# Operands of the seven products formed once and kept in DRAM, gate's elementwise work on VectorE, and a block's final norm in the next block

## The chip, the cores and the metric

One core of one Trainium2 chip. The metric is device time in microseconds of one execution of the program; the time given for the kernel before is the median of three runs. The engines are named as in the profile: PE (TensorE: matmuls; PEld is its weight loads), DVE (VectorE), ACT (ScalarE), POOL (GpSimd) and SP (SyncE, which here issues every DMA). Each engine runs its own instructions in order and waits on semaphores for the others.

## The reference

One layer of a streaming encoder over 2048 prompt frames and 64 frames of a running stream, model width 1024, feed-forward width 2816, all in float32. Retention heads and forgetting-attention heads work on one input projection; their outputs meet in one output projection. What matters here is what follows it:

```python
x = x + jnp.einsum('btc,cd->btd', mix, w_out)
h = _rmsnorm(x, g_ffn)
g = jnp.einsum('btd,df->btf', h, w_gate)
u = jnp.einsum('btd,df->btf', h, w_up)
x = x + jnp.einsum('btf,fd->btd', jax.nn.silu(g) * u, w_down)
y = _rmsnorm(x, norm_final_gain)
```

for 2048 + 64 frames.

## The kernel before

**Precision.** A float32 matrix is kept as two parts, `hi` (a cast on ACT) and `lo` (the rest, a subtraction on DVE); the helper `split` (L83) issues both. A product is three matmuls: hi·hi, hi·lo, lo·hi. Since `split` is a helper, all casts stand at L85 and all subtractions at L86 of the profile; the tile names tell them apart. All DMAs are issued in `dma`, L48, on SP's queue.

**Seven products.** Gate and up, `h @ w_gate` and `h @ w_up`, are not formed with eight products of half-size blocks but with seven, in the manner of Strassen and Winograd. The tokens of a block are cut into two halves, the 1024 input features into two halves, and a weight's columns into two halves. From the quarters b11, b12 (first 512 features, first and second half of the tokens), b21, b22 (the other 512 features) seven right-hand operands are made: b11, b12 - b11 = t1, b22 - t1 = t2, b22 - b12, t2 - b21, b21 and b22; from the weight's quarters seven left-hand operands likewise (`prep`, L1068). The seven results are added up in PSUM and on DVE into the four quarters of the output.

**Stages.** The program first runs the input projection and both kinds of heads. Then comes the *output projection* (`p3_stream`): a loop over 17 tiles of 128 tokens (the last has 64). For tile i it loads the mixer's output `m` and the softmax sums `rb`, splits them, does 48 matmuls with the resident `w_out`, adds `x`, stores the sum as `x1_d`, forms the norm `h`, and one tile later (`back`, L550) transposes `h` eight times on PE into `hT` (bufs 2), which is stored as one 512 KB piece in `h2_d`. It is interleaved with attention up to about 1432 us and runs alone from there to about 1581 us.

Beside its second half, `prefetch` (L1044) brings the operands of the first FFN block into SBUF: in four steps, each of which loads two pieces of `h2_d`, forms t1, t2 and two differences on DVE and POOL (L1023 to L1030), and splits the seven operands for one of four groups of 128 features into `hb`, which holds all seven operands, hi and lo. A step is issued when a given tile of the output projection has been issued (`p3_done`: 6, 8, 10, 12; then the first weights at 14). Its buffers are the two of tag `raw` in pool `ws`, which the output projection's `m` and `rb` use too.

The *FFN* goes over three blocks of 768, 768 and 576 tokens (`BLOCKS`), and in each over 11 passes (`NP`) of 256 of the 2816 columns. Pass i is

- gate, `gu(i, 0)`: seven products of 12 matmuls each; `prep` is called four products ahead and makes the weights' operands: three sums when a weight tile is new (L1079 to L1081), one more at the fourth product (L1084), all on POOL, and a split for each product;
- down of the pass before, `down(i - 1)`: for each half of the 1024 output columns, for each tile of 128 tokens, six matmuls and an addition to `y` on DVE (L1183);
- up, `gu(i, 1)`: as gate; its outputs are multiplied with gate's `G` and split into `act`, the input of down.

In `out` (L1125) a quarter of up's output is finished in four links: DVE adds PSUM to a partial sum (L1134), POOL multiplies with `G` (L1135), ACT casts to `act`, DVE subtracts. The first product of each gate or up part is copied out of PSUM by ACT (L1156); the third accumulates on the same PSUM buffer and must wait for that copy.

In the last pass of a block the operands of the next block are loaded and formed as in `prefetch`, from four buffers, and then the last down runs; its second half ends for each tile with `finish` (L1188): the final norm (square and sum on ACT, two small operations on POOL, scale on DVE), the output's DMA. `hb` has one buffer, so the new operands are written after the last product of the old block. The next block's `y` tiles (6 buffers) are loaded after its first gate part.

The order of the instructions on each engine is laid out by the framework when the program is built: it may move an instruction ahead of one written earlier where its inputs and its buffer are there sooner. So in the trace the next block's first gate products stand between the matmuls of the last down.

Of the kernel before, what the change touches and what calls it, by code (L numbers as in the profile page):

```python
# [16 lines left out]
D = 1024  # L17
# [21 lines left out]
def hybrid_kernel(ctx: ExitStack, tc: tile.TileContext, a: dict):  # L39
# [18 lines left out]
    h2_d = tc.dram_tile([128, KT, TP], F32, name="h2_d")  # L58
# [449 lines left out]
    def p3_stream(last):  # L508

        m_t, mT_t, x_t, h_t, rb_t = {}, {}, {}, {}, {}  # L510

# [38 lines left out]
        def back(i):  # L550
# [8 lines left out]
            dma(h2_d[:, :, i * 128:(i + 1) * 128], hT)  # L559
            p3_done.add(i)  # L560

# [443 lines left out]
    def load_h(n, raws):  # L1005

        t0, nt = BLOCKS[n]
        hf = nt // 2
        hb = hb_t[n] = hp.tile([128, 7, 2, 4, HALF], F32R, tag="hb", name="hb")
        for k in range(4):  # L1010
            r = []
            for e in range(2):
                raw = raws()[:, 0:nt]
                dma(raw, h2_d[:, 4 * e + k, t0:t0 + nt])
                r += [raw[:, 0:hf], raw[:, hf:nt]]
            b11, b12, b21, b22 = r
            t1 = hp.tile([128, HALF], F32, tag="t1", name="t1")[:, 0:hf]
            t2 = hp.tile([128, HALF], F32, tag="t2", name="t2")[:, 0:hf]

            def put(j, src):  # L1020
                split(hb[:, j, 0, k, 0:hf], hb[:, j, 1, k, 0:hf], src)

            ve.tensor_tensor(t1, b12, b11, op=ALU.subtract)  # L1023
            ge.tensor_tensor(b12, b22, b12, op=ALU.subtract)
            ve.tensor_tensor(t2, b22, t1, op=ALU.subtract)
            put(0, b11)
            put(2, b21)
            put(4, t1)
            put(1, t2)
            ge.tensor_tensor(b21, t2, b21, op=ALU.subtract)  # L1030
            put(3, b12)
            put(6, b22)
            put(5, b21)
            yield
# [9 lines left out]
    def prefetch():  # L1044

        for n, _ in enumerate(load_h(0, lambda: ws.tile([128, D], F32, tag="raw", name="raw"))):
            yield 8 + 2 * n
        load_w(0, 0, ws)
        yield 14
# [9 lines left out]
    with tc.tile_pool(name="fw", bufs=1, reuse_waits="tile") as fw, \  # L1059
# [8 lines left out]
        def prep(x):  # L1068
# [6 lines left out]
            if j == 0:  # L1075
# [3 lines left out]
                ge.tensor_tensor(s1, r1[:, lo], r1[:, hi], op=ALU.add)  # L1079
                ge.tensor_tensor(s2, s1, r0[:, lo], op=ALU.subtract)  # L1080
                ge.tensor_tensor(r1[:, lo], r0[:, lo], r1[:, lo], op=ALU.subtract)  # L1081
# [205 lines left out]
```

## Time and profile before

| | |
|---|---|
| median of three runs | 3120.7 us (3119.35 to 3123.26) |
| the profiled execution | 3118.12 us, its span 3116.3 us |
| granted TensorE clock, mean | 0.984 |
| instructions | 45009 |
| output projection alone on the chip | about 1436 to 1581 us |
| FFN, first and last gate or up matmul | 1580.7 to 3086 us |

In the profile, a line of the timeline has the start, the duration (in us), the engine, the line of the kernel, the operation and its output and inputs by name; in brackets the idle time of that engine just before and what ended it. A row of a stretch (A:B) has the stretch's length and the busy time of each engine with its number of instructions, then the granted clock, the share of DMA time and GB/s. A row of a group has the number of instructions, their total, the mean in ns, and the idle time before them with its cause.

### The profile page before, as it was taken

What the parts mean: (1) busy time and instruction counts of PE and PEld (TensorE: products, weight loads), DVE (VectorE), ACT (ScalarE), POOL (GpSimd) and SP (SyncE); (2) the same over time, 40 slices, a digit from 0 to 9 for tenths busy, and PEclk for the clock granted to TensorE, in tenths of its full rate; (3) what the DMA queues carried; (4) which work ended last, traced back from release to release, by engine and by line L of the source; (5) the groups of instructions that cost most, each with busy time, mean ns of one, the idle gap of its engine ahead of it and who ended that gap; (6) DMA issues with size and microseconds to landing.
All of it is one profiled execution on the core that took longest, in us unless ns stands there. A gap on an engine that the chain in (4) does not pass through costs nothing. (4 is left out here: it accounts for less than half of the span.)

```text
span 3116.3 us, 45009 instructions
## 1 busy us (share of the span) xinstructions
PE 2953.4 (95%) x16684; PEld 2645.7 (85%) x16684; DVE 1976.0 (63%) x3661; ACT 1252.3 (40%) x2662; POOL 707.6 (23%) x804
## 2 busy tenths in 40 slices
PE   8999899999999999898889999998999999899997
PEld 8999778788888888777679998987888998788886
DVE  4233554477766677665446766769666676877776
ACT  4233332265655556554332322324233233433332
POOL 0000111111111111000132323324233232433332
PEclk9999999999999999999989999999999999899999
DMA  7565633332422223544652222225212221522221
GB/s 200 168 183 169 172 97 108 100 104 77 131 84 72 60 85 118 155 123 137 188 176 62 68 68 61 75 61 170 81 55 74 64 66 56 168 82 83 87 82 51
DMA packets 415261, 328.91 MB, mean 106 GB/s; under 512 B 22346, under 2 KB 361674, under 8 KB 415042
## 3 DMA queue, kind: packets, MB, share of 16 engines
q1 hardware_dynamic: 415042, 326.05, 34.9%
q8 instruction: 131, 2.15, 0.3%
q14 instruction: 88, 0.72, 0.1%
HBM read 246.81 MB, written 79.17 MB: 105 GB/s over the span
## 5 line engine op out<-in xcount | busy, mean ns | idle before, releaser
L1153 PE MATMUL mm<-hb,w 128*128 128x384 f32 (+1 forms) x5544 | 926.8, 327 | 75.5 <-ACT U L1156 45.4
L1153 PEld LDWEIGHTS mm<-hb,w 128*128 128x128 f32 x5544 | 903.2, 191 | 98.8 <-ACT U L1156 54.3
L1182 PE MATMUL dn<-wd,act 128*128 128x512 f32 (+1 forms) x2244 | 518.8, 391 | 4.4 <-ACT act L85 3.9
L1182 PEld LDWEIGHTS dn<-wd,act 128*128 128x128 f32 (+1 forms) x2244 | 413.4, 185 | 99.7 <-ACT act L85 5.6
L492 PE MATMUL mm<-w,hT 128*128 128x512 f32 x1632 | 445.8, 408 | 0.7 <-DVE hT L86 0.5
L86 DVE TENSOR_TENSOR w<-raw,w 128x512 fp32r<-128x512 f32 (+1 forms) x358 | 346.4, 988 | 80.2 <-ACT w L85 76.9
L1183 DVE TENSOR_TENSOR y<-y,dn 128x512 f32<-128x512 f32 (+1 forms) x374 | 255.5, 686 | 202.8 <-PE dn L1182 202.5
L492 PEld LDWEIGHTS mm<-w,hT 128*128 128x128 f32 x1632 | 291.3, 190 | 56.3 <-issue 2.2
L232 PE MATMUL mm<-w,hT 128*128 128x386 f32 x1632 | 298.8, 342 | 0.9 <-ACT hT L85 0.9
L85 ACT CAST w<-raw 128x512 fp32r<-128x512 f32 (+1 forms) x358 | 220.6, 643 | 195.2 <-PE mm L1153 98.5
L232 PEld LDWEIGHTS mm<-w,hT 128*128 128x128 f32 x1632 | 288.6, 190 | 1.9 <-ACT hT L85 1.5
L85 ACT CAST wd<-rawd 128x512 fp32r<-128x512 f32 x132 | 75.4, 618 | 394.0 <-PE dn L1182 381.3
L872 ACT ACTIVATE P<-P,nm 128x512 f32<-128x512 f32 (+3 forms) x288 | 189.6, 661 | 96.2 <-DVE nm L866 95.9
L567 PE MATMUL mm<-w,mT 128*128 128x512 f32 x816 | 210.3, 407 | 3.1 <-ACT mT L85 1.8
L86 DVE TENSOR_TENSOR lo<-t,hi 128x512 fp32r<-128x512 f32 (+1 forms) x288 | 183.0, 655 | 44.2 <-ACT hi L85 42.4
L85 ACT CAST hi<-t 128x512 fp32r<-128x512 f32 (+1 forms) x288 | 154.6, 562 | 139.8 <-PE t L889 136.0
L567 PEld LDWEIGHTS mm<-w,mT 128*128 128x128 f32 x816 | 152.8, 193 | 36.6 <-ACT mT L85 2.2
L1135 POOL TENSOR_TENSOR G<-G,T 128x384 f32<-128x384 f32 (+1 forms) x33 | 32.7, 992 | 627.0 <-DVE T L1134 627.0
L889 PE MATMUL t<-ident,P 128*128 128x128 f32 x1088 | 160.1, 276 | 15.3 <-DVE lo L86 9.1
L86 DVE TENSOR_TENSOR act<-G,act 128x384 fp32r<-128x384 f32 (+1 forms) x132 | 133.9, 1014 | 51.0 <-ACT act L85 50.3
L889 PEld LDWEIGHTS t<-ident,P 128*128 128x128 f32 x1088 | 128.3, 142 | 37.0 <-DVE lo L86 13.8
L377 POOL TENSOR_TENSOR qk<-t,t 128x256 f32<-128x256 f32 x34 | 24.8, 729 | 592.2 <-DVE t L374 285.4
(231 smaller groups left out, 4060.5 us busy)
## 6 DMA issues: line engine op xcount, KB each, us to landing
raw<-w_gate SPq DMA_DIRECT2D x66, 512.0 KB
raw<-w_up SPq DMA_DIRECT2D x66, 512.0 KB
rawd<-w_down SPq DMA_DIRECT2D x66, 512.0 KB
hf<-hT_d SPq DMA_DIRECT2D x34, 512.0 KB
qk_d<-qkT SPq DMA_DIRECT2D x32, 512.0 KB
KA<-qk_d SPq DMA_DIRECT2D x72, 128.0 KB
V<-v_d SPq DMA_DIRECT2D x36, 256.0 KB
hT_d<-hf SPq DMA_DIRECT2D x17, 512.0 KB
```

Source lines behind the costliest of these rows:

```text
L85: se.copy(hi, src)
L86: ve.tensor_tensor(lo, src, f32(hi), op=ALU.subtract)
L232: te.matmul(ps, hT[:, u, k], w[:, v, k], start=n == 0, stop=n == 23)
L377: ge.tensor_tensor(qk[:, :, 0], t1[:, :, 0], t2[:, :, 1], op=ALU.subtract)
L492: te.matmul(ps, hT[:, u, k], w[:, v, k], start=k == 0 and j == 0, stop=k == 7 and j == 2)
L567: te.matmul(ps, mT[:, u, k], mix_w[4 + c][:, v, k], start=k == 0 and j == 0, stop=k == 7 and j == 2)
L872: se.activation(v, v, AF.Exp, bias=nm, scale=-1.0, accum_out=sum_t[h, u // 4][:, i % 8, ch:ch + 1])
L889: te.transpose(tr[:, c * 128:(c + 1) * 128], P_t[n, e, j // 2][:, k * 128:(k + 1) * 128], ident)
L1135: ge.tensor_tensor(g, g, x if q != 3 else T, op=ALU.mult)
L1153: te.matmul(ps, w[:, u, k], hb[:, j, v, k, 0:hf], start=b == j and k == 0 and m == 0, stop=j not in (0, 4) and k == 3 and m == 2, skip_gro ...
L1182: te.matmul(ps, act_t[i][e][:, u, s], w[:, v, e], start=e == 0 and j == 0, stop=e == 1 and j == 2)
L1183: ve.tensor_tensor(y[:, d], y[:, d], ps, op=ALU.add)
```

## The change

1. The quarters' differences are formed in the output projection. After every second tile, `operands` takes the two transposed tiles (the first is the "first half", the second the "second half"), forms t1, t2 and the two differences for all 512 features at once (three DVE operations and one POOL operation on 512 columns) and stores the seven operands as seven 256 KB pieces of `h2_d`, now `[7, 128, 4, 1152]`. The last tile, of 64 tokens, is cut into two of 32. A block's halves are so the even and the odd tiles, and `tiles(n)` and `act` follow this order; in block 2 (halves of 288) a quarter of `act` is split in two pieces.
2. `load_h` only loads (14 pieces of 2 x 384 columns, 393 KB) and splits. In `prefetch` the 14 steps are spread over the tiles from 6 to 14; the first weights are asked for after tile 15.
3. The products with `G` (L1135) go from POOL to DVE; of the weights' sums, gate's three and both fourth ones go to DVE, up's three stay on POOL.
4. In `down` the loop over tiles is outside and that over the two halves of the columns inside. At a block's end the splits of the next operands are written between the tiles of the last down, and `finish` of the old block and `load_y` of the new one are written into the next gate part, one tile per product. In the last block `finish` follows each tile of down. The first block's `y` is loaded ahead of the passes.

```diff
-    h2_d = tc.dram_tile([128, KT, TP], F32, name="h2_d")
+    h2_d = tc.dram_tile([7, 128, 4, 9 * 128], F32, name="h2_d")
...
-            dma(h2_d[:, :, i * 128:(i + 1) * 128], hT)
+            hT_b.append(hT)
+            if i == NT - 1:
+                operands(i // 2, hT[:, :, 0:NS // 2], hT[:, :, NS // 2:NS])
+            elif i % 2:
+                operands(i // 2, *hT_b[-2:])
             p3_done.add(i)
+
+        def operands(j, b1, b2):
+
+            w = b1.shape[2]
+            lo, hi = slice(0, 4), slice(4, 8)
+            t = (p3.tile([128, D], F32, tag="h", name="t", bufs=1).rearrange("p (k t) -> p k t", k=KT) if j == NT // 2 else
+                 ws.tile([128, KT, 128], F32, tag="raw", name="t"))[:, :, 0:w]
+
+            def out(n, src):
+                dma(h2_d[n, :, :, j * 128:j * 128 + w], src)
+
+            out(0, b1[:, lo])
+            out(2, b1[:, hi])
+            out(6, b2[:, hi])
+            ve.tensor_tensor(t[:, lo], b2[:, lo], b1[:, lo], op=ALU.subtract)
+            ve.tensor_tensor(t[:, hi], b2[:, hi], t[:, lo], op=ALU.subtract)
+            ve.tensor_tensor(b2[:, lo], b2[:, hi], b2[:, lo], op=ALU.subtract)
+            out(4, t[:, lo])
+            out(1, t[:, hi])
+            out(3, b2[:, lo])
+            ge.tensor_tensor(b1[:, hi], t[:, hi], b1[:, hi], op=ALU.subtract)
+            out(5, b1[:, hi])
...
+        def load(x):
+            raw = raws()[:, 0:2 * hf].rearrange("p (k t) -> p k t", k=2)
+            j, k = divmod(x, 2)
+            dma(raw, h2_d[j, :, 2 * k:2 * k + 2, c0:c0 + hf])
+            raw_h.append(raw)
+
+        yield load
+        for x in range(14):
+            j, k = x // 2, x % 2 * 2
+            split(hb[:, j, 0, k:k + 2, 0:hf], hb[:, j, 1, k:k + 2, 0:hf], raw_h[x])
+            yield None
...
-        for n, _ in enumerate(load_h(0, lambda: ws.tile([128, D], F32, tag="raw", name="raw"))):
-            yield 8 + 2 * n
+        g = load_h(0, lambda: ws.tile([128, D], F32, tag="raw", name="raw"))
+        load = next(g)
+        for x in range(14):
+            load(x)
+            next(g)
+            yield 8 + x // 2 if x < 13 else 15
         load_w(0, 0, ws)
...
+                en = ge if s else ve
+                en.tensor_tensor(s1, r1[:, lo], r1[:, hi], op=ALU.add)
+                en.tensor_tensor(s2, s1, r0[:, lo], op=ALU.subtract)
+                en.tensor_tensor(r1[:, lo], r0[:, lo], r1[:, lo], op=ALU.subtract)
             if j == 3:
-                ge.tensor_tensor(r0[:, hi], r0[:, hi], s2, op=ALU.subtract)
+                ve.tensor_tensor(r0[:, hi], r0[:, hi], s2, op=ALU.subtract)
...
-                    ge.tensor_tensor(g, g, x if q != 3 else T, op=ALU.mult)
+                    ve.tensor_tensor(g, g, x if q != 3 else T, op=ALU.mult)
...
-            for c in range(2):
-                d = slice(c * 512, (c + 1) * 512)
-                w = wd_t.pop((i, c))
-                for t, s in tiles(n):
+            w = [wd_t.pop((i, c)) for c in range(2)]
+            for t, m, f in tiles(n):
+                y = y_t[t][0:m]
+                for c in range(2):
...
+            old = [x[0:2] for x in tiles(n - 1)] if n and not p else []
+            new = [x[0:2] for x in tiles(n)]
             for j in gu(i, 0):
...
+                if old:
+                    finish(*old.pop(0))
+                    if new:
+                        load_y(*new.pop(0))
...
+            if p == NP - 1 and n + 1 < NB:
...
+                for x in range(4):
+                    load(x)
+                todo = down(i)
+                for x in range(14):
+                    next(g)
+                    if x + 4 < 14:
+                        load(x + 4)
+                    if x % 2 and x > 1:
+                        next(todo)
...
+            elif p == NP - 1:
+                for t, m in down(i):
+                    finish(t, m)
```

More of the change, by code (lines that the diff above doesn't have):

```diff
@@ L510, in p3_stream @@
         m_t, mT_t, x_t, h_t, rb_t = {}, {}, {}, {}, {}
+        hT_b = []
         def load_m(i):
@@ L1005, in load_h @@
     def load_h(n, raws):
-        t0, nt = BLOCKS[n]
-        hf = nt // 2
+        hf = BLOCKS[n][1] // 2
+        c0 = BLOCKS[n][0] // 2
         hb = hb_t[n] = hp.tile([128, 7, 2, 4, HALF], F32R, tag="hb", name="hb")
[L1010 to L1034, printed above, removed]
+        raw_h = []
+        def load(x):
[8 more added lines that the diff above has]
+            yield None
     def load_w(i, s, pool):
@@ L1103, in tiles, with load_y @@
             t0, nt = BLOCKS[n]
-            return [(t0 + t, slice(t, min(t + 128, nt))) for t in range(0, nt, 128)]
-        def load_y(n):
-            for t, s in tiles(n):
-                y = y_t[t] = fw.tile([128, D], F32, tag="y", name="y", bufs=6)
-                dma(y[0:s.stop - s.start], x1_d[t:t + s.stop - s.start])
+            hf, tail = nt // 2, nt % 128
+            full = [(t0 + 128 * m, 128, m // 2 * 128 + m % 2 * (hf + tail // 2)) for m in range(nt // 128)]
+            return full + ([(t0 + nt - tail, tail, hf - tail // 2)] if tail else [])
+        def load_y(t, m):
+            y = y_t[t] = fw.tile([128, D], F32, tag="y", name="y", bufs=6)
+            dma(y[0:m], x1_d[t:t + m])
         def gu(i, s):
@@ L1119, in gu @@
             else:
-                act_t[i] = [fw.tile([128, 2, BLOCKS[0][1]], F32R, tag="act", name="act", bufs=2) for _ in range(2)]
+                act_t[i] = [fw.tile([128, 2, 2 * HALF], F32R, tag="act", name="act", bufs=2) for _ in range(2)]
             G = G_t[i]
@@ L1202, in hybrid_kernel @@
                     split_d(i - 1, j // 4)
-            if p == 0:
-                load_y(n)
-            else:
-                down(i - 1)
+                if old:
+                    finish(*old.pop(0))
+                    if new:
+                        load_y(*new.pop(0))
+            if p:
+                for _ in down(i - 1):
+                    pass
             for j in gu(i, 1):
@@ L1212, in hybrid_kernel @@
                     split_d(i, j // 4)
-            if p == NP - 1:
-                if n + 1 < NB:
-                    ring = [lambda: rup.tile([128, D], F32, tag="raw", name="raw"),
-                            lambda: fw.tile([128, D], F32, tag="rawd", name="rawd", bufs=2)]
-                    pick = [ring[e] for _ in range(2) for e in (0, 0, 1, 1)]
-                    for _ in load_h(n + 1, lambda: pick.pop(0)()):
-                        pass
-                    load_w(i + 1, 1, rup)
-                down(i)
+            if p == NP - 1 and n + 1 < NB:
+                ring = [lambda: rup.tile([128, D], F32, tag="raw", name="raw"),
+                        lambda: fw.tile([128, D], F32, tag="rawd", name="rawd", bufs=2)]
+                pick = [ring[x % 4 // 2] for x in range(14)]
+                g = load_h(n + 1, lambda: pick.pop(0)())
+                load = next(g)
+                for x in range(4):
[7 more added lines that the diff above has]
+                        next(todo)
+                for _ in todo:
+                    pass
+                load_w(i + 1, 1, rup)
+            elif p == NP - 1:
+                for t, m in down(i):
+                    finish(t, m)
 def constants():
```

29 lines of the change are left out of this document (15 added, 14 removed).

## The prediction

> **What bounds the kernel now.** I read the page's totals first, then stretches of the span cut where the stages change, then the waits and one pass in order of time.
>
> ```profile
> span 3116.3 us, 45009 instructions
> PE 2953.4 (95%) x16684; PEld 2645.7 (85%) x16684; DVE 1976.0 (63%) x3661; ACT 1252.3 (40%) x2662; POOL 707.6 (23%) x804
> ```
>
> TensorE (PE) is busy for 95% of the span, so a gain can only come from the 163 us in which it waits. Where these lie (columns: stretch, its length, busy time of PE, weight loads, VectorE, ScalarE, GpSimd):
>
> ```profile
> 1436.00:1545.00 109.00, 92.20 (x410) 72.82 (x409) 55.20 (x79) 38.60 (x72) 14.88 (x22) 0.97 0.58 179
> 1545.00:1580.70 35.70, 35.70 (x167) 28.74 (x166) 11.92 (x15) 9.77 (x17) 3.15 (x7) 1.00 0.52 165
> 1580.70:1606.50 25.80, 17.81 (x82) 15.84 (x80) 10.84 (x15) 9.63 (x17) 10.82 (x10) 0.78 0.75 229
> 1606.50:2102.20 495.70, 478.76 (x2495) 447.41 (x2496) 339.86 (x472) 156.82 (x298) 160.35 (x117) 0.99 0.24 73
> 2102.20:2185.00 82.80, 67.50 (x321) 58.90 (x321) 74.91 (x101) 40.04 (x81) 39.51 (x37) 0.94 0.53 171
> 2185.00:2644.30 459.30, 444.40 (x2326) 413.26 (x2324) 315.87 (x439) 141.09 (x268) 143.04 (x105) 1.00 0.22 65
> 2644.30:2717.00 72.70, 59.08 (x315) 51.50 (x314) 64.46 (x99) 36.56 (x81) 34.87 (x36) 0.87 0.55 172
> 2717.00:3087.80 370.80, 355.72 (x2210) 320.37 (x2208) 273.49 (x416) 129.94 (x265) 128.23 (x102) 0.99 0.26 76
> 3101.30:3116.30 15.00, 0.02 (x1) 0.00 (x0) 5.80 (x6) 3.45 (x6) 2.20 (x6) 0.59 0.40 147
> ```
>
> Length less PE's time gives PE's idle: output projection after attention 16.8 and 0.0; entry to the FFN 8.0; passes of block 0 16.9; change to block 1 15.3; passes of block 1 14.9; change to block 2 13.6; passes of block 2 15.1; end 15.0. The diff touches all of these: 115 us.
>
> A pass of block 1, at the seam between up's last product and the next gate:
>
> ```profile
> 2267.37 0.55 DVE L1134 TENSOR_TENSOR U<-U,mm 128x384 f32<-128x384 f32 x1
> 2267.99 1.38 POOL L1135 TENSOR_TENSOR G<-G,U 128x384 f32<-128x384 f32 x1 [1.68 <-DVE U L1134]
> 2269.40 0.51 ACT L85 CAST act<-G 128x384 fp32r<-128x384 f32 x1 [1.50 <-POOL G L1135]
> 2269.82 0.47 ACT L1156 COPY U<-mm 128x384 f32<-128x384 f32 x1
> 2270.35 10.67 PE L1153 MATMUL mm<-hb,w 128*128 128x384 f32 x60 [1.67 <-ACT U L1156]
> ```
>
> PE stands 1.67 us for a copy that ScalarE (ACT) could have made earlier: it is queued behind a cast that waits for GpSimd's product. That is nearly all the idle of blocks 0 and 1.
>
> ```profile
> 2233.26:2249.55 16.29, 16.29 (x74) 13.51 (x74) 9.66 (x15) 1.67 (x3) 3.85 (x3) 1.00 0.10 33
> 2222.91:2270.34 47.43, 45.77 (x240) 42.63 (x240) 32.60 (x46) 14.75 (x29) 15.06 (x12) 1.00 0.23 67
> 2977.10:2984.20 7.10, 6.59 (x48) 6.36 (x48) 7.10 (x10) 2.57 (x5) 4.76 (x4) 1.00 0.50 148
> 2977.10:3015.10 38.00, 36.33 (x229) 32.84 (x229) 28.64 (x44) 13.80 (x29) 14.01 (x12) 1.00 0.28 84
> ```
>
> Down's part (first row) and the whole pass (second) of block 1: VectorE (DVE) has 32.6 of 47.4 us, and 22.9 of the 31.1 outside down. In block 2 the pass takes 38.0, and its first 7.1 us are already full on DVE.
>
> **The change, part by part.**
>
> *Gate's products and weight sums to DVE.* Clean and contended prices (columns: busy, mean ns):
>
> ```profile
> L86 DVE TENSOR_TENSOR w<-raw,w 128x512 fp32r<-128x512 f32 x285 | 274.3, 985 | 46.0 <-ACT w L85 43.9
> L86 DVE TENSOR_TENSOR w<-s,w 128x512 fp32r<-128x512 f32 x114 | 80.4, 705 | 2.3
> L1081 POOL TENSOR_TENSOR raw<-raw 128x512 f32<-128x512 f32 x57 | 87.8, 1541 | 0.0
> L1137 DVE TENSOR_TENSOR G<-G,mm 128x384 f32<-128x384 f32 x1 | 0.6, 554 | 1.4 <-PE mm L1153 1.4
> ```
>
> Per pass DVE gets three products (0.55 each), three sums of the gate's weights and two of L1084 (0.7 each): 5.2 us. GpSimd keeps the three sums of up's weights, 3 x 1.5 = 4.6 of its 15.1 us. DVE's subtractions that run beside GpSimd take 985 ns on average where the same shape takes 705; ten per pass make 2.8 us, of which about two thirds should go. DVE: 32.6 + 5.2 - 2 = 36 us, and PE's need is 47.4 - 1.7 = 45.7.
> At the seam the link from DVE's U to the cast is now 1.48 us (2267.92 to 2269.40) and becomes one DVE product and a handover, 0.6; the link before it, for V, shortens likewise and U stands behind it on DVE. Against this, T's and V's products and one L1084 enter DVE's queue ahead of U, 1.8 us, into slack that the contended subtractions leave. U's copy then starts about 2.5 us earlier than now, and 1.7 is what the stall takes; late next is the last weight subtraction ahead of U on DVE, about 0.25 us per pass. Blocks 0 and 1: 31.8 us of idle less 20 x 0.25 is **-27** (bounds -31 and +10, the latter if DVE's queue holds PE 0.5 us a pass more than today's wait).
> *Block 2.* PE's need is 36.3 us a pass. DVE gets 3 x 0.45 + 5 x 0.7 = 4.9 and two extra small subtractions, 0.4, where the 576 tokens no longer divide into tiles. 28.6 + 5.3 - 2 = 32 of 36.3, and the first 7 us are full today and keep GpSimd's three sums beside them. I take a third of the 15.1: **-5** (bounds -15 and +20).
> *Down's loops swapped.* Same matmuls; both halves of w_down must be split before the first tile, and all four of its casts now wait for the end of the previous down. They have a whole gate part (14 us) as cover: 0. If it is gone, four casts, 2.5 us a pass.
> *Block changes.* The two rows are those of the elements of `hb` alone, then of `t`, in the two changes:
>
> ```profile
> 2090.00:2185.00 95.00, 62.96 (x320) 57.87 (x319) 17.02 (x28) 12.87 (x28) 0.95 0.50 162
> 2632.00:2717.00 85.00, 54.64 (x314) 50.58 (x313) 14.21 (x28) 10.52 (x28) 0.89 0.50 158
> 2090.00:2185.00 95.00, 0.00 (x0) 0.00 (x0) 12.65 (x16) 4.09 (x8) 4.92 (x4) 0.95 0.50 162
> ```
>
> DVE bounds a change (74.9 of 82.8 us). Out go 28 subtractions of 17.0 us and the eight of L1023 and L1025 (12.65 less the eight `hb<-t` at 0.6 to 0.75, so 7); in come 14 of double width, by 705 ns for 512 columns about 1.05 each, 14.7. Net -9, in block 2 about -8; the moved operations of two gate/up parts give back 5 less relief. The final norms move into the next gate and up parts, which hide them: 0. If they do not, six stand there at the 3.1 us each of the end's norms (below), 18 us. Fourteen loads of 393 KB replace eight, in a stretch at half DMA share: 0. Together **-12** of 28.9 (bounds -24 and +18).
> *End.*
>
> ```profile
> 3096.68 1.06 ACT L91 ACTIVATE o<-y 128x1024 f32<-128x1024 f32 x1 [6.68 <-DVE y L1183]
> 3109.01 1.06 ACT L91 ACTIVATE o<-y 64x1024 f32<-64x1024 f32 x1 [3.03 <-DMA o_yp<-o]
> ```
>
> Five norms start from 3096.7 to 3109.0, 3.1 us each, held by two output buffers. With the tile loop outside, the first starts after one fifth of down (3087.8 to 3101.3), at about 3091; the last at 3091 + 4 x 3.1 = 3104: -5, taken as **-4** (bounds -7 and 0).
> *Output projection.* Seven stores of 256 KB per two tiles replace two of 512 KB; three DVE and one GpSimd operation per two tiles lie in DVE's idle (55 of 109 us busy). SP issues 63 stores where it had 17, and four of seven wait for DVE or GpSimd with x's and the mixer's loads queued behind them; that is part of the upper bound. The prefetch loses its elementwise chain but makes 14 loads, not 8, in the two `ws` buffers that it shares with the next mixer tile and now with `t`.
>
> ```profile
> L85 ACT CAST hb<-raw 128x384 fp32r<-128x384 f32 x20 | 9.9, 511 | 16.6 <-DMA raw<-h_d 11.1 <-POOL raw L1030 4.6 <-POOL raw L1024 0.8
> PE rt L556 <- ACT hT L557: 15.1, 5, 4.7
> ```
>
> PE waits because ACT, in order, sits on casts of prefetched data: five waits, 15.1 us. ACT waited 11.1 us for eight loads, 1.4 each; 14 make 19.4, so **+4** (bounds: -15, all gone; +27, fourteen waits of 3.0). The traffic is the second reason for a plus. 0.58 of DMA time moved 179 GB/s, so full use is about 309. Two tiles need 1.8 (stores) + 1.6 (four loads) + 1.05 (mixer) + 0.5 (row sums) + 2.1 (x in and out) = 7.1 MB in 2 x 12.0 us (35.7 us hold 167 of 56 matmuls a tile): 296 GB/s, 96%.
> By the Trainium skill, "DMA: Bandwidth & Descriptors", Specifications, HBM gives one core about 358 GB/s; by that these 296 would be 83%, and the term would be 0 and not +4. No run here shows 358.
> *Entry.* The first weights are asked for one tile later, and the last 64-token tile has seven small stores.
>
> ```profile
> 1590.02 0.52 SPq L48 DMA_DIRECT2D h_d<-hT  x1
> 1593.85 1.01 SPq L48 DMA_DIRECT2D raw<-w_up  x2
> ```
>
> The loads of w_up stand behind that store on SP's queue; six more at 0.5 us and a GpSimd result make **+4** (bounds: -3, four sums that DVE does 0.8 us faster each; +12, weights late by a tile). The block's `y` loads move ahead of the passes; down needs them a gate and an up part later: 0.
>
> **Sum.** -27 - 5 - 12 - 4 + 4 + 4 = -40. The profiled execution took 3118.1 us (1.8 beyond its span), the median shown is 2.6 above that: 3078 on the profiled one, 3080 on the median.
>
> **Rivals.**
> - *DVE becomes the bound (slower).* Place: gate/up of block 2 and the block changes, where DVE is full today. What decides is whether the moved work fits: without relief from GpSimd block 2 needs 28.6 + 5.3 = 33.9 of PE's 36.3 us on an engine that works in order and in down's part waits for PE at each addition to `y`. If that costs 2 us a pass, block 2 loses 20; the changes then give 0, blocks 0 and 1 give 10, and with -4 + 4 + 4 it is +14: 3134. Against it: the relief, 2.8 us of excess a pass in `w<-raw` alone. The kernel is slower than now once DVE's waits exceed the forecast's by 40 / 33 = 1.2 us a pass.
> - *The stall only changes its name (the change doesn't do what it says).* ACT's U copy comes in time, but DVE's later operations hold PSUM buffers as long: passes stay at 47.4 and 38.0, and -12 - 4 + 8 leaves 3113. For it: block 2 has such waits; against: block 1 has none besides U's.
> - *Prefetch swamps the output projection.* +27 and +12 in place of +4 and +4: 3112. For it: 96% of the traffic the trace shows possible and two buffers; against: after 1545 there was no idle at all to begin with.
> - *All stalls go.* Passes -42, changes -24, end -6, projection -10, entry 0: 3039.
>
> **How the numbers follow.** Forecast 0.55, DVE bound 0.15, renamed stall 0.10, swamped projection 0.12, all gone 0.08. The forecast's own range is 3055 (15 more from the passes and 10 from the changes) to 3103 (the swamped projection's 23 alone). Leaving out the DVE case's 0.15 beyond its near edge and the extreme of the last case, 3045 to 3122 holds 8 in 10. A change of 0.2%, 6 us, is what this kernel's runs can tell. Faster: nearly all of the forecast and of the last case, three quarters of the two middle ones, 0.79; same 0.06; slower 0.15.
>
> **What would show it.** Right: no wait of PE on L1156's copy in blocks 0 and 1, passes at 45.5 to 46 us, GpSimd under 6 us a pass, DVE's `w<-raw` mean near 800 ns, the last norm near 3064. Wrong: PE waiting for DVE in block 2 with passes over 38 us; tiles of the output projection over 14 us; w_up landing more than 8 us later against the last projection.

## The result, and the profile after

| | before | after |
|---|---|---|
| median | 3120.0 us (3116.5 to 3123.3) | 3052.9 us (3049.1 to 3054.0) |
| ratio after to before | | 0.978, 95% interval 0.977 to 0.980 |
| span of the profiled execution | 3116.3 us | 3052.1 us |

The kernel is 2.2% faster: 67 us where 40 were forecast. The time is 27 us below the predicted one, inside the wide range (3045 to 3122) and 2 us below the forecast's own (3055 to 3103). That it lies inside is in part luck: the sum hides two errors that cancel in part. The FFN gained far more than forecast, and the output projection lost five to seven times what was put down for it.

The page's totals:

```profile
span 3052.1 us, 44866 instructions
PE 2940.8 (96%) x16684; PEld 2644.4 (87%) x16684; DVE 1998.9 (65%) x3908; ACT 1253.6 (41%) x2642; POOL 379.4 (12%) x525
```

GpSimd (POOL) lost 328 us of busy time and VectorE (DVE) took on only 23, since the operations that came to it were nearly made up for by others that became shorter or went out. The stretches of the same stages, with the columns of the prediction's (length, busy time of PE, weight loads, VectorE, ScalarE, GpSimd; clock, DMA share, GB/s), and under them single passes of block 1 and block 2:

```profile
1426.90:1602.60 175.70, 144.48 (x595) 111.50 (x595) 68.20 (x91) 46.67 (x76) 16.65 (x27) 0.90 0.60 182
1602.60:1628.40 25.80, 17.78 (x82) 15.73 (x80) 13.60 (x22) 9.84 (x16) 7.00 (x7) 0.87 0.96 281
1628.40:2114.50 486.10, 484.10 (x2544) 453.89 (x2545) 361.23 (x576) 166.19 (x310) 52.64 (x30) 1.00 0.26 78
2114.50:2180.00 65.50, 59.16 (x308) 55.34 (x307) 58.26 (x84) 31.64 (x57) 17.71 (x18) 0.97 0.71 223
2180.00:2635.00 455.00, 455.00 (x2396) 424.93 (x2395) 338.34 (x538) 154.96 (x290) 46.97 (x30) 1.00 0.26 74
2635.00:2690.00 55.00, 48.79 (x295) 44.34 (x294) 47.36 (x77) 24.49 (x51) 16.27 (x15) 0.94 0.64 202
2690.00:3025.00 335.00, 331.51 (x2109) 302.21 (x2108) 278.33 (x485) 129.68 (x277) 47.51 (x27) 1.00 0.28 82
...
2206.46:2251.97 45.51, 45.51 (x242) 42.70 (x241) 33.43 (x54) 14.85 (x29) 5.11 (x3) 1.00 0.25 70
...
2737.06:2773.48 36.42, 36.03 (x230) 32.79 (x229) 30.55 (x54) 14.14 (x31) 5.31 (x3) 1.00 0.29 87
```

PE's idle is length less PE's time. In the passes of block 1 it is nothing at all, in block 0 it is 2.0 us and in block 2 3.5 (before: 14.9, 16.9, 15.1). The two changes of block keep 6.3 and 6.2 of 15.3 and 13.6. The first row runs from the last matmul of attention to the last of the output projection. The same stretch of the kernel before:

```profile
1432.17:1580.70 148.53, 131.73 (x595) 104.76 (x595) 67.94 (x96) 48.92 (x90) 18.02 (x29) 0.98 0.55 171
```

It is 27.2 us longer now. Only 14.4 of that are idle (31.2 for 16.8): the other 12.8 are the same 595 matmuls taking longer, at a granted clock of 0.90 for 0.98.

The whole span, cut at fixed instructions (the last attention matmul, the last projection matmul, and the copies of the first product, L1156 before and L1182 after, which come at the same place of every pass), adds up to it:

| stage (us) | before | after | difference |
|---|---|---|---|
| up to the last attention matmul | 1432.2 | 1426.9 | -5.3 |
| output projection after it | 148.5 | 175.7 | +27.2 |
| entry, first pass | 51.2 | 48.3 | -2.9 |
| block 0, 9 passes | 428.6 | 409.6 | -18.9 |
| change to block 1, 3 passes | 162.0 | 145.9 | -16.1 |
| block 1, 8 passes | 379.5 | 364.1 | -15.3 |
| change to block 2, 3 passes | 147.2 | 130.1 | -17.2 |
| block 2, 8 passes | 303.5 | 291.4 | -12.2 |
| last pass and end | 63.8 | 60.1 | -3.6 |
| sum | 3116.3 | 3052.1 | -64.2 |

A pass takes 45.51 us where it took 47.45, and in block 2 36.42 where it took 37.94 (medians). The first row varies among executions of the same code: 1432 to 1436 us for before and the two below that form operands as before does (e3, e4), 1426 to 1431 for after and the eight below that store them on SP's queue as after does (e1, e2, e5, e6, e9 to e12). The two groups do not overlap, so a part of the -5.3, perhaps all of it, belongs to the change, and its loss up to the projection's end lies between 21.9 and 27.2.

### The profile page after: what moved, and what is told of

It is laid out like the page before. It is cut to its first block, busy times and chain, and to the rows that moved or that the text cites. A ratio compares the mean times of both kernels' runs of the same rounds, so it can differ in the third digit from the quotient of the medians.

```text
span 3052.1 us, 44866 instructions
## 1 busy us (share of the span) xinstructions
PE 2940.8 (96%) x16684; PEld 2644.4 (87%) x16684; DVE 1998.9 (65%) x3908; ACT 1253.6 (41%) x2642; POOL 379.4 (12%) x525
## 3 DMA queue, kind: packets, MB, share of 16 engines
q1 hardware_dynamic: 438594, 338.76, 37.5%
## 5 line engine op out<-in xcount | busy, mean ns | idle before, releaser
L1179 PE MATMUL mm<-hb,w 128*128 128x384 f32 (+1 forms) x5544 | 905.6, 324 | 21.8 <-DVE G L1152 13.9
L1179 PEld LDWEIGHTS mm<-hb,w 128*128 128x128 f32 x5544 | 895.3, 189 | 31.2 <-issue 13.1
L86 DVE TENSOR_TENSOR w<-raw,w 128x512 fp32r<-128x512 f32 (+1 forms) x358 | 313.2, 888 | 52.2 <-ACT w L85 46.2
L492 PEld LDWEIGHTS mm<-w,hT 128*128 128x128 f32 x1632 | 291.4, 190 | 56.3 <-issue 2.2
L594 PE MATMUL mm<-w,mT 128*128 128x512 f32 x816 | 221.1, 420 | 14.2 <-ACT mT L85 13.2
L594 PEld LDWEIGHTS mm<-w,mT 128*128 128x128 f32 x816 | 157.8, 201 | 53.2 <-ACT mT L85 17.5
L1099 POOL TENSOR_TENSOR s<-raw 128x512 f32<-128x512 f32 x33 | 68.6, 2079 | 1058.2 <-DVE w L86 1023.8
L932 PE MATMUL pv<-hi,V 128*128 128x256 f32 x576 | 153.4, 292 | 1.6 <-DVE o L941 0.8
L882 DVE TENSOR_SCALAR_CACHE_REDUCE P<-s 128x512 f32<-128x512 f32 x192 | 129.6, 684 | 30.6 <-PE s L879 26.2
```

What stands on the lines that cost most here:

```text
L86: ve.tensor_tensor(lo, src, f32(hi), op=ALU.subtract)
L492: te.matmul(ps, hT[:, u, k], w[:, v, k], start=k == 0 and j == 0, stop=k == 7 and j == 2)
L594: te.matmul(ps, mT[:, u, k], mix_w[4 + c][:, v, k], start=k == 0 and j == 0, stop=k == 7 and j == 2)
L882: ve.tensor_scalar(o, ps, 1.0, None, op0=ALU.mult, op1=ALU.min, accum_out=m)
L932: te.matmul(o, V, hi[:, p], start=j == 0 and c == 0, stop=False)
L1179: te.matmul(ps, w[:, u, k], hb[:, j, v, k, 0:hf], start=b == j and k == 0 and m == 0, stop=j not in (0, 4) and k == 3 and m == 2, skip_gro ...
```

## The experiments

### What the passes gained from: e1, e2, e10

These three start from the kernel after and give work back to GpSimd.

e1, the products with `G`:

```diff
-                    ve.tensor_tensor(g, g, x if q != 3 else T, op=ALU.mult)
+                    ge.tensor_tensor(g, g, x if q != 3 else T, op=ALU.mult)
```

> The changed kernel with only the products with G (L1135 of the kernel before) put back on GpSimd; the weight sums stay on VectorE. Theory 'seam' (PE's stall per pass is ScalarE's copy of U queued behind the cast that waits for GpSimd's product): passes of blocks 0 and 1 return to 47.0 to 47.5 us, those of block 2 to 37.5 to 38, the time to about 3053 + 21 x 1.9 + 10 x 1.4 = 3107. Rival 'port' (the stall came from VectorE's subtractions slowed beside GpSimd's weight sums, and the products' engine hardly matters): passes stay at 45.5 to 46 and 36.4 to 36.8, time 3053 to 3063.

e10, the weights' sums alone:

```diff
-                en = ge if s else ve
+                en = ge
...
-                ve.tensor_tensor(r0[:, hi], r0[:, hi], s2, op=ALU.subtract)
+                ge.tensor_tensor(r0[:, hi], r0[:, hi], s2, op=ALU.subtract)
```

> The kernel after with the weights' sums alone back on GpSimd; the products with G stay on DVE. Giving back the products alone returned 1.31 of the 1.94 us of a pass in blocks 0 and 1 (46.82), giving back both 47.44. Theory A (the products at the seam are the cause, the sums only contention): a pass of 45.6-46.2 us, of block 2 36.6-37.3, 3058-3075. Theory B (either one alone brings back most of the stall): passes of 46.8 or more, 3095-3105. Theory C (only the products matter): 45.5, 3050-3056.

e2, both edits:

> The changed kernel with the products and all weight sums put back on GpSimd; operands in DRAM, the loops of down and the moved final norms stay. 'Seam': passes 47.4 and 37.9, the same as with only the products back, 3107. 'Port': passes 47.4 and 37.9 here too, but not with the products alone. If the order of down or the moved norms had made part of the passes' gain: passes below 47.

| | median us | ratio to before (95%) | pass, blocks 0 and 1 | pass, block 2 |
|---|---|---|---|---|
| after | 3052.9 | 0.978 (0.977 to 0.980) | 45.51 | 36.42 |
| e1, products on GpSimd | 3101.6 | 0.994 (0.993 to 0.996) | 46.82 | 37.46 |
| e10, sums on GpSimd | 3070.4 | 0.983 (0.982 to 0.985) | 45.51 | 37.64 |
| e2, both on GpSimd | 3120.7 | 1.000 (0.999 to 1.001) | 47.44 | 38.10 |

With both given back the passes are those of before, and so is the time: without the engines' part the rest of the change brings nothing. In blocks 0 and 1 the sums alone cost nothing, the products alone 1.31 us a pass, both 1.93. That bears out the passes of e10's third theory there. In block 2 neither alone is harmless, so no single theory held for all blocks: e10's time, 3070.4, lies in the range of its first theory, and its passes do not. e1 lies between its two theories: 46.82 and 37.46 are a little short of the seam's 47.0 to 47.5 and 37.5 to 38, and far from the rival's. e2 came 14 us above the 3107 of its first theory: the whole stall needs the sums on GpSimd too, as its second had it.

The seam of a pass in block 1, of the kernel after (start, duration, engine, line, operation; in brackets the idle before):

```profile
2293.74 5.04 PE L1179 MATMUL mm<-hb,w 128*128 128x384 f32 x28
...
2295.56 0.55 DVE L1156 TENSOR_TENSOR U<-U,mm 128x384 f32<-128x384 f32 x1
...
2296.49 0.55 DVE L1157 TENSOR_TENSOR G<-G,U 128x384 f32<-128x384 f32 x1
2296.96 0.69 DVE L86 TENSOR_TENSOR w<-s,w 128x512 fp32r<-128x512 f32 x1
2297.08 0.51 ACT L85 CAST act<-G 128x384 fp32r<-128x384 f32 x1 [0.45 <-DVE G L1157]
2297.50 0.47 ACT L1182 COPY U<-mm 128x384 f32<-128x384 f32 x1
```

and of e1:

```profile
2368.27 0.55 DVE L1156 TENSOR_TENSOR U<-U,mm 128x384 f32<-128x384 f32 x1
2368.73 0.69 DVE L86 TENSOR_TENSOR w<-s,w 128x512 fp32r<-128x512 f32 x1
2368.96 1.33 POOL L1157 TENSOR_TENSOR G<-G,U 128x384 f32<-128x384 f32 x1 [1.74 <-DVE U L1156]
2369.34 1.50 DVE L86 TENSOR_TENSOR w<-raw,w 128x512 fp32r<-128x512 f32 x1
...
2370.32 0.51 ACT L85 CAST act<-G 128x384 fp32r<-128x384 f32 x1 [1.51 <-POOL G L1157]
2370.74 0.47 ACT L1182 COPY U<-mm 128x384 f32<-128x384 f32 x1
...
2371.26 0.44 PE L1179 MATMUL mm<-hb,w 128*128 128x384 f32 x1 [1.01 <-ACT U L1182]
```

From U's end to the cast's start it is 0.97 us in the first (2296.11 to 2297.08) and 1.50 in the second, and only in the second does PE wait for the copy behind the cast. The subtraction that runs beside GpSimd there (2369.34) takes 1.50 us; one of the same shape in the kernel after (2296.96), with GpSimd idle, 0.69. The one that had begun before GpSimd's product did (2368.73) took 0.69 as well.

Why the sums matter in block 2, from the groups of e10, then of after (number, total us, mean ns), and a wait of PE in block 2 in e10 (total us, times, longest):

```profile
L1157 DVE TENSOR_TENSOR G<-G,U 128x288 f32<-128x288 f32 x11 | 15.0, 1362 | 0.0
```

```profile
L1157 DVE TENSOR_TENSOR G<-G,U 128x288 f32<-128x288 f32 x11 | 5.0, 453 | 0.0
```

```profile
PE mm L1179 <- DVE G L1152: 11.0, 8, 1.4
```

One such product in e10, in order of time, with the sum beside it:

```profile
2743.65 1.46 POOL L1099 TENSOR_TENSOR s<-raw 128x512 f32<-128x512 f32 x1 [2.43 <-DVE w L86]
2743.86 1.56 DVE L1157 TENSOR_TENSOR G<-G,U 128x288 f32<-128x288 f32 x1
```

Beside GpSimd's sum of gate's weights DVE's last product takes three times as long. Nine of the eleven in e10 stand so and take 1.56 to 1.57 us; the other two meet no sum and take 0.45 to 0.46. In the kernel after, PE's same wait is 0.4 us in each pass of block 2, 3.1 us in eight.

### What each part of the change brought: e3, e4

e3 is the kernel before with part 3 alone (the engines). e4 has in addition the swapped loops of `down`, the final norms and the `y` loads at their new places; it still forms the operands from `hT` when they are loaded.

e3, on the kernel before:

```diff
-                ge.tensor_tensor(s1, r1[:, lo], r1[:, hi], op=ALU.add)
+                en = ge if s else ve
+                en.tensor_tensor(s1, r1[:, lo], r1[:, hi], op=ALU.add)
...
-                ge.tensor_tensor(r0[:, hi], r0[:, hi], s2, op=ALU.subtract)
+                ve.tensor_tensor(r0[:, hi], r0[:, hi], s2, op=ALU.subtract)
...
-                    ge.tensor_tensor(g, g, x if q != 3 else T, op=ALU.mult)
+                    ve.tensor_tensor(g, g, x if q != 3 else T, op=ALU.mult)
```

> The kernel before with only the products and weight sums moved to VectorE as in the change; operands formed at the block changes, norms and loops as before. 'Seam': passes 45.5 and 36.4, so -19 -15 in blocks 0 and 1, -12 in block 2, and some 5 in the seams of the two block changes: 3120 - 51 = 3069, output projection ending near 1581. Rival (block 2 and the changes need the operations that the operands in DRAM take off VectorE): block 2 stays at 37 to 38 and the changes lose what VectorE gets: 3085.

e4, on e3, among others:

```diff
-            for c in range(2):
...
-                for t, s in tiles(n):
+            for t, s in tiles(n):
...
+                for c in range(2):
...
-                    if c and i % NP == NP - 1:
-                        finish(t, y)
```

> The kernel before with the engines' part and with down's loops swapped and the final norms and y loads moved as in the change; operands still formed at the block changes from the stored transposed tiles. If the 23 us that the two block changes gained beyond their seams come from the operands in DRAM: about 3069 - 4 (end) = 3065. If they come from the moved norms: about 3045. The output projection ends near 1581 in both (the changed kernel: 1603).

| us | before | e3 | e4 | after |
|---|---|---|---|---|
| median | 3120.0 | 3056.5 | 3055.1 | 3052.9 |
| output projection | 148.5 | 152.3 | 151.6 | 175.7 |
| change to block 1 | 162.0 | 155.0 | 156.8 | 145.9 |
| change to block 2 | 147.2 | 138.9 | 135.1 | 130.1 |
| last pass and end | 63.8 | 63.8 | 60.4 | 60.1 |

The ratios to before are 0.980 (0.978 to 0.981) and 0.979 (0.978 to 0.981). The engines' part, a few lines, gives nearly the whole gain. That is more than e3 was expected to give (3069): its passes are as its first theory had them (45.51, and 36.7 in block 2 for 36.4), but the two changes gained 15.3 us for the 5 put down, and the entry to the FFN 5.1. e4 lies between its two values, 3065 and 3045. The loops' order gives 3.4 us at the end; the moved norms are worth +1.8 at one change and -3.7 at the other, which is nothing that these runs can tell. The operands in DRAM take 10.9 and 5.1 us off the two changes, and the projection takes 24 us longer; its end comes 14.7 us later, since attention ends 9.4 us earlier than in e4's profiled execution. So the stored operands as they stand here bring about nothing: what they save is paid for one stage earlier.

### Where the output projection lost it: e5 to e9, e11, e12

In the kernel after, waits in that stretch (engine, line waited for: us in total, times, longest):

```profile
PE rt L557 <- ACT hT L558: 12.5, 4, 4.5
PE mm L594 <- ACT mT L85: 11.9, 7, 3.3
...
SPq L48 <- DVE hb L86: 16.9, 12, 4.1
SPq L48 <- DVE mT L86: 16.3, 5, 7.4
```

Before, PE had no wait on mT there; it now has seven, 11.9 us. The two rows of SP's queue are transfers that wait for a buffer of `ws` until a split has read it. One tile in order of time shows the link:

```profile
1502.04 1.71 SPq L48 DMA_DIRECT2D raw<-h_d  x2
...
1503.81 0.54 SPq L48 DMA_DIRECT2D x_d<-x  x1
...
1507.01 0.83 ACT L85 CAST hb<-raw 128x768 fp32r<-128x768 f32 x1 [4.92 <-DMA raw<-h_d]
1507.87 0.96 DVE L86 TENSOR_TENSOR hb<-raw,hb 128x768 fp32r<-128x768 f32 x1 [2.96 <-ACT hb L85]
...
1508.86 0.36 SPq L48 DMA_DIRECT2D m<-mix_d  x1
1509.06 0.96 DVE L86 TENSOR_TENSOR hb<-raw,hb 128x768 fp32r<-128x768 f32 x1 [0.23 <-ACT hb L85]
...
1510.04 1.29 SPq L48 DMA_DIRECT2D rb<-rsum_d  x2
```

Two prefetched operands take both buffers from 1502.0 on. After the store of the sum (1503.81) SP's queue stands still for 4.5 us: the next mixer tile `m` is asked for when the first operand is split (1508.86), `rb` when the second is (1510.04). Two buffers serve `m`, `rb`, `t` and 14 operands.

Edits of the kernel after test this. e5 gives the prefetched operands two buffers of their own:

```diff
-        g = load_h(0, lambda: ws.tile([128, D], F32, tag="raw", name="raw"))
+        g = load_h(0, lambda: own.tile([128, 2 * HALF], F32, tag="pre", name="raw"))
...
+    own = own_st.enter_context(tc.tile_pool(name="own", bufs=2, side="right", reuse_waits="tile"))
```

> The changed kernel, but the 14 loads that prefetch block 0's operands have two buffers of their own (3 KB per partition each) instead of sharing the two of ws with the mixer's tiles and t. Theory 'ring' (the output projection grew from 148.5 to 175.7 us after attention because mixer tiles, row sums, t and prefetched operands take turns in two buffers, and SP, in order, stands until one is free): 150 to 158 us, total 3053 - 20 = 3033. Theory 'traffic' (the stores and loads, 24% more, fill the DMA engines): stays at 172 to 177, total 3050 to 3055.

e6 gives only `t` a buffer of its own:

```diff
-                 ws.tile([128, KT, 128], F32, tag="raw", name="t"))[:, :, 0:w]
+                 p3.tile([128, KT, 128], F32, tag="t", name="t", bufs=1))[:, :, 0:w]
```

> The changed kernel, but t, the buffer for two of the differences, has a buffer of its own instead of one of ws. 'Ring': of some nine takings of a buffer per two tiles this removes one, which is held for three DVE operations and three stores: projection 165 to 172 us, total 3043 to 3050. 'Traffic': 172 to 177, total as the changed kernel.

e7 issues the operands' stores on GpSimd's queue, e8 does so on top of e5:

```diff
-                dma(h2_d[n, :, :, j * 128:j * 128 + w], src)
+                ge.dma_start(h2_d[n, :, :, j * 128:j * 128 + w], src)
```

> The changed kernel, but the operands' stores are issued on GpSimd's DMA queue, so that a store that waits for a difference no longer holds up the loads behind it on SP. Theory 'SP order': SP's waits for t and hT (14 us of 67 in the last 120 us of the projection) go, and the projection falls by about 10 to 165 us, total 3043. 'Ring': SP still waits for buffers, at most 5 us less. 'Traffic': unchanged or slower by the other queue's descriptor work.

> Both: own buffers for the prefetch, and the stores on GpSimd's queue. 'Ring' alone: as with the buffers alone (3033), within 4 us. If SP's order adds to it: projection near 150 us and 3025 to 3030. 'Traffic': 172 to 177, 3053.

After these, e11 adds to e6 a buffer for `rb` (2 KB per partition), and e12 has one buffer for the prefetched operands and one for `rb`:

```diff
-                rb = ws.tile([128, KT, 128], F32, tag="raw", name="rb")[:, 0:4]
+                rb = p3.tile([128, 4, 128], F32, tag="rb", name="rb", bufs=1) if i else ws.tile([128, KT, 128], F32, tag="raw", name="rb")[:, 0:4]
```

> The kernel after with t and the row sums rb in buffers of their own (one each), so that the two of `ws` hold only the mixer tiles and the prefetched operands. It was 156.1 us of output projection and 3043.1 us with t alone outside. In that kernel PE's remaining idle there stands before the transposes, for ACT's hT copy, and ACT stands before a cast that waits for the product with rb. Theory A (the row sums' load is late because it waits for a buffer): rb is there early, the projection falls to 142-150 us, the time to 3026-3037. Theory B (the load is late because SP's queue is held by stores and prefetched loads ahead of it, whatever buffer it has): 153-159 us, 3040-3047. Theory C (mixer tile and operands now alternate more closely in the two buffers, and the mixer tile comes late): 160 us and more, over 3047.

> The kernel after with one buffer of its own for the prefetched operands, and one for the row sums rb; `ws` holds mixer tiles and t. With two own buffers for the operands and rb in `ws` it was 154.0 us of output projection and 3034.7 us. Theory A (the row sums' buffer is what is late): 142-152 us and 3023-3033, since 14 operands have 10 tiles of 12 us and one buffer carries a load and its split in about 6 us. Theory B (SP's queue, in order, is held by a load that waits for its one buffer): 158-170 us, 3039-3052. No change if neither matters: 153-156 us, 3034-3037.

| us | median | ratio to before (95%) | output projection | PE's idle | PE busy | clock |
|---|---|---|---|---|---|---|
| before | 3120.0 | | 148.5 | 16.8 | 131.7 | 0.98 |
| after | 3052.9 | 0.978 (0.977 to 0.980) | 175.7 | 31.2 | 144.5 | 0.90 |
| e5 own two for operands | 3034.7 | 0.973 (0.972 to 0.975) | 154.0 | 17.5 | 136.5 | 0.93 |
| e6 own one for t | 3043.1 | 0.975 (0.974 to 0.977) | 156.1 | 20.9 | 135.2 | 0.96 |
| e7 stores on GpSimd | 3061.8 | 0.981 (0.980 to 0.983) | 174.6 | 31.9 | 142.7 | 0.91 |
| e8 e5 and e7 | 3057.8 | 0.980 (0.978 to 0.982) | 168.9 | 30.8 | 138.1 | 0.91 |
| e11 own for t and rb | 3027.4 | 0.970 (0.969 to 0.971) | 145.1 | 12.4 | 132.7 | 0.96 |
| e12 one for operands, one for rb | 3026.4 | 0.970 (0.969 to 0.971) | 147.4 | 14.5 | 132.9 | 0.97 |

The stretch of e11, with the same 595 or 596 matmuls and the same loads and stores:

```profile
1428.85:1573.93 145.08, 132.73 (x596) 105.66 (x595) 69.02 (x92) 45.82 (x76) 17.79 (x27) 0.96 0.71 217
```

Its waits for the mixer tile, and those of e6, which differs only in the buffer of `rb`. First e6:

```profile
DVE m L537 <- DMA rb<-rsum_d: 34.8, 8, 7.3
ACT mT L85 <- DVE m L537: 26.3, 6, 7.2
```

Then e11:

```profile
DVE m L537 <- DMA rb<-rsum_d: 16.0, 4, 7.9
...
ACT mT L85 <- DVE m L537: 2.2, 1, 2.2
```

Sharing the two buffers is the cause: e5, e6 and e12 each take other tiles out of them, and each time most of the loss is gone (e6 was expected to win far less, 165 to 172 us; the count of takings, one in nine, was no measure of what a taking costs); with `t` and `rb` out (e11) the projection takes 145 us, shorter than before the change, though it issues 63 stores for 17. e6 and e11 together separate two links: `t` is worth 20 us of the projection, `rb` 11 more, and the second is a wait that the kernel before had too (32.1 us of DVE for `rb`, eight times). Theory A, that the row sums are late for want of a buffer, held in e11 and e12; e12's rival, a queue held by the single buffer of the operands, did not. With these buffers the stored operands do pay: e11 is some 28 us under e4. How much of that is `rb`'s own buffer, which the kernel before and e4 could have too, was not tried.

Traffic is excluded as the cause: the kernel after moved 182 GB/s in that stretch, e11 217 in less time. e11 and e12 agree within their ranges (3025 to 3031, 3024 to 3031) and are the fastest versions here, 0.8 to 0.9% under the kernel after. Two own buffers for the operands, one for `t` and one for `rb` together were not tried.

e7 and e8 turned the wrong way: the theories with a gain had 3043 for e7 and 3025 to 3037 for e8. In e7 the projection alone takes as long as after's, and attention, beside which its first half runs, ends 10.5 us later (1437.4); in e8 11.6 us later than in e5 (1439.5 for 1427.9). GpSimd's waits in e7, after attention's end:

```profile
POOL h_d L575 <- ACT hT L558: 67.3, 12, 11.4
...
POOL h_d L575 <- DVE t L580: 43.8, 5, 13.2
```

GpSimd stands 111 us before stores whose data are not ready, in order with the small operations of the norm (L93, L95) that the next tile needs. The stores' waits, which SP's queue had borne, now stand ahead of work that the next tile waits for; this is read from the waits, no run takes it apart. e8 lost 15 of the 22 us that e5 had won in the projection.

e9 was meant to take the mixer tile's split out of the way of ACT's copies in e5, by writing it two groups of matmuls later.

```diff
-                        if (c, q) == (1, 0) and 0 < i < NT - 1:
+                        if (c, q) == (1, 2) and 0 < i < NT - 1:
                             halves(i + 1)
```

> The kernel after with the own two buffers for the prefetch, and the mixer tile's splits (`halves`) written two groups of matmuls later, behind the transposes of `back` and not ahead of them. With the own buffers the output projection still has three waits of PE for ACT's hT copy, 13 us in all, because the copy stands on ACT behind the cast of the mixer tile, and that waits for the row sums' load. Theory A (order on ACT is what remains): the projection falls from 154 to 141-146 us and the time from 3034.7 to 3022-3027. Theory B (the load itself is late, so PE waits for the mixer tile instead): the wait changes its name, 152-156 us, 3032-3037. Theory C (the split now comes so late that the next tile's first matmul waits for it): 160 us or more, over 3040.

It measured 3039.7 us, 0.974 (0.973 to 0.975), projection 156.4. It tells nothing of its theories: the framework lays out the same instructions in the same order on every engine as for e5. So the two are executions of the same order of work, and 3034.7 and 3039.7 show by how much two such medians differ, 0.16%.

## Why the prediction was right, and where it was not

**Passes of blocks 0 and 1, -27: mechanism right, too small.** A pass gains 1.94 us; the 17 in the table's two rows give -34.2, so the 20 counted by the prediction come to about -39. There is no wait of PE on the copy, the passes take 45.51 (forecast 45.5 to 46), GpSimd has 5.1 us a pass (under 6). The 0.25 us that was to be late next never came, 5 us; and the 45.77 us of PE's busy time in a pass, taken as PE's need, became 45.51, another 5.

**Block 2, -5: too small.** Its eight passes between the changes gave -12.2. "A third of the 15.1" supposed that DVE stays close to full. It has 30.6 of 36.4 us where 32 of 36.3 were worked out, so there was room. The relief was there, if smaller than forecast: the mean of DVE's `w<-raw` fell from 985 to 888 ns (forecast near 800; the two means are over different stretches of the program). e10 shows that in this block the sums had to leave GpSimd as well.

```profile
L86 DVE TENSOR_TENSOR w<-raw,w 128x512 fp32r<-128x512 f32 (+1 forms) x358 | 313.2, 888 | 52.2 <-ACT w L85 46.2
```

**Block changes, -12: too small.** Idle fell from 28.9 to 12.5 us, -16.4. In time the six passes of the table's two rows gained 33.3; less 10.8 for what six such passes gain elsewhere (an estimate, 4 x 1.94 and 2 x 1.52) that is 22.5. Beside the idle the granted clock rose, which the sum had left out: 0.97 and 0.94 where it was 0.94 and 0.87. How much each gave was not taken apart. That the operands' elementwise work leaves a stretch that DVE bounds was right: DVE's busy time in the two stretches fell from 139 us for 636 matmuls to 106 for 603. Norms hidden, and fourteen loads for eight at no cost, were right too.

**End, -4, and loops swapped, 0: right.** -3.6 and, of all waits of down's matmuls in the program, 3.1 us for a cast of w_down. The last norm starts at 3044.8, not near 3064, because the whole kernel ends earlier than forecast.

```profile
L1208 PE MATMUL dn<-wd,act 128*128 128x512 f32 (+1 forms) x2244 | 518.3, 390 | 3.1 <-ACT wd L85 3.1
```

**Output projection, +4: this step failed.** It measured +27.2 from attention's end, +21.9 at its own. The sign named for it came too: a tile took 16.5 us (175.7 us for 595 matmuls of 56 a tile), over the 14 named. But it was 14.0 before as well; the 12.0 of the prediction are from the last 36 us, which have no wait. Three things went into the error.
- "ACT waited 1.4 us for each of eight loads; 14 make 19.4" priced a load at ACT's old wait for it, and the +4 seems to be these 19.4 less PE's 15.1, two different waits. The price of a load here is how long it holds one of two buffers that `m` and `rb` need, and that was named ("in the two `ws` buffers that it shares") without being worked out. One load to a freed buffer took 6.8 us (1502.04 to 1508.86), against 12 us of a tile.
- Only stalls were counted. Stalls are followed by a lower clock (last section), and the matmuls' longer time was 12.8 of the 27.2 us.
- Traffic, "296 GB/s, 96%", was no reason. The stretch had 182 GB/s; e11 moved the same bytes at 217. The 309 GB/s for full use was worked out from a mean, and a share does not fix a rate: 6 us of the kernel before have 331 at a share of 0.95, which would be 348 in full, and 6 us of the kernel after have 270 at 1.00 (last section).

```profile
1440.00:1446.00 6.00, 6.00 (x27) 4.87 (x26) 3.79 (x6) 2.68 (x7) 1.05 (x3) 1.00 0.95 331
```

  The Trainium skill ("DMA: Bandwidth & Descriptors", Specifications) gives about 358 for one core, and the 348 of this row are near it. By the page the term would have been 0, further off than +4, because the term did not hang on the rate.

The upper bound of the term, +27, is what came, but by another working: it was fourteen waits of 3.0 us for casts, and the trace has seven new waits for the mixer tile and a slower clock.

**Entry, +4: wrong sign, -2.9.** The seven small stores do stand ahead of `w_up`, but it is asked for (at 1614.74) 12.1 us after the last projection matmul, and was 13.2 us before; PE's idle in the first 25.8 us is 8.0 in both. The table's row holds the first pass too. e3 and e4, without the stored operands, have 46.1 us there: so the engines' part gave -5.1, of which 1.9 is what any pass gains, and the stored operands +2.2 (the row is 48.3 in after and 47.3 to 49.5 in the five kernels below that differ from it in buffers alone). With the stores on GpSimd's queue (e7, e8) it is 44.3 and 44.8. So the plus for the stores was there, at half its size. What outweighed it is not the faster sums, as the lower bound had it: with the sums back on GpSimd (e10) the row is 47.3, with the products back (e1) 50.7.

**The rivals.** DVE as the bound did not come; DVE fits, since what left GpSimd made DVE's other work shorter. The renamed stall did not come either: block 1 has no idle. Swamping the projection came in full in that stage and not at the entry, and it did not decide, since the passes and changes gave more. "All stalls go" was the nearest for the passes (-42; about -51 came) and in time, though not in idle, for the changes (-24), and wrong for the projection. The predicted 3080 lies above the result because the table's rows of the blocks and their changes gained 79.7 us where 44 were put down, and that outweighs the projection.

## What to carry to other kernels

When a prefetch gets more and smaller pieces, count the buffers and not the bytes: list every tile that takes a buffer of that pool, in the order of the queue, and how long each holds it; two buffers, of 4 and 2 KB per partition, were worth 25 us here (e11). Price stalls of TensorE with the slow clock after them, in this stage nearly as much again (12.8 us beside 14.4). When an elementwise link at a seam waits for another engine, moving that small product can be worth more than restructuring the stage around it (e3 and e4 here), and what it does beside the other moved operations has to be tried with and without them (e1, e2, e10).

## What was not expected of the hardware

**Short gaps halve the clock for a while.** Matmuls of one shape on PE in the projection of the kernel after, in order of time (a row's duration is that of all its matmuls), and the granted clock of some stretches among them:

```profile
1498.81 7.38 PE L594 MATMUL mm<-w,mT 128*128 128x512 f32 x31
...
1509.98 7.38 PE L594 MATMUL mm<-w,mT 128*128 128x512 f32 x23
1519.25 6.69 PE L594 MATMUL mm<-w,mT 128*128 128x512 f32 x21 [1.89 <-ACT mT L85]
```

```profile
1500.00:1506.00 6.00, 6.00 (x27) 4.80 (x26) 2.74 (x4) 1.15 (x2) 2.15 (x3) 1.00 1.00 270
...
1508.00:1510.00 2.00, 0.43 (x5) 0.44 (x5) 1.77 (x2) 1.32 (x2) 0.00 (x0) 1.00 0.30 120
1510.00:1512.00 2.00, 2.00 (x9) 1.62 (x7) 0.01 (x1) 0.59 (x1) 0.00 (x0) 0.64 0.98 282
1512.00:1514.00 2.00, 1.90 (x5) 0.93 (x4) 0.67 (x2) 0.62 (x1) 0.00 (x0) 0.51 0.85 295
1514.00:1516.00 2.00, 2.00 (x10) 1.61 (x9) 0.62 (x2) 1.15 (x2) 0.04 (x1) 1.00 0.20 62
```

Before the first gap a matmul takes 238 ns (7.38 over 31). PE then waits 2.0 us (up to 1509.6), and the next 23 take 321 on average, those at 1519, after another 1.9 us, 319. These averages mix two speeds: the trace grants the clock in full or by half, and by half from 1510.54 to 1513.96 and from 1520.78 to 1524.20, 3.41 us each; there a matmul starts about 425 ns after the one before it, outside of it about 235. In this stage of both kernels each such stretch begins right after 3.41 us of which PE was idle for 1.87 or more; where the clock stayed full it was at most 1.82. The kernel before has 6.8 us of half clock in the stage, the kernel after 34.1, and half of the difference, 13.7, is about the 12.8 us that the matmuls took longer. The Trainium skill, "TensorE: Matmul & The Clock Gate", Part 1, has the clock fall after an idle window of about 3.4 us. Here 3.41 us that were idle for little more than half were enough.

**GpSimd and VectorE slow each other, and it depends on what meets and on which begins first.** DVE's 128x288 product is 453 ns alone and 1565 beside GpSimd's sums (e10). In the kernel before, the 125 subtractions of 128x512 for the weights that begin while an elementwise operation of GpSimd runs take 1.48 us in the median; the 66 that GpSimd joins after their start take at most 0.69, as those that it does not touch. GpSimd's first sum of a weight tile (L1099) takes 2079 ns on average in the kernel after and 1676 in e1, for the same 512 columns; the one in after with VectorE idle takes 1315.

**A store on GpSimd's queue takes GpSimd's own time.** In e7 the 26 stores of `hT` keep it busy for 770 ns each, beside the waits shown above.

```profile
L575 POOL DMA_DIRECT2D h_d<-hT x26 | 20.0, 770 | 69.2 <-ACT hT L558 67.3 <-POOL hT L586 1.5 <-issue 0.4
```
